# A hybrid decoder layer in three-way split fp32 on one core: first weight blocks between the tiles of x, parameter rows and gates moved ahead, another split of the last sum

## The chip, the core and the metric

One Trainium2 chip, of which the program uses one core. The time is the device time of one execution in microseconds (us), the median over the runs shown; lower is better.

## What is computed

One decoder layer on x (512 x 1024, fp32), followed by a final RMSNorm. Three mixers share one input projection; then come an output projection, a gated MLP with a causal convolution, and the norm.

```python
h = rms_norm(x, attn_norm_w[i])
g_q, g_k, g_v, g_z, g_b, g_a, s_u, d_q, d_k, d_v = split_cols(h @ w_in[i], IN_SIZES)
qkv = jax.nn.silu(causal_dwconv(jnp.concatenate([g_q, g_k, g_v], axis=-1), gdn_conv_w[i]))
...
log_decay = (-jnp.exp(gdn_a_log[i]) * jax.nn.softplus(g_a + gdn_dt_bias[i]))
o_gdn = gated_delta_chunked(l2norm(g_q), l2norm(g_k), g_v, beta, log_decay)   # gated DeltaNet, 4 heads
...
# s5_mixer: per group, s_t = Lbar s_{t-1} + Bbar u_t, y_t = Re(C s_t) + D u_t; GELU; GLU
lam_bar = jnp.exp(lam * dt)
b_bar = ((lam_bar - 1.0) / lam)[..., None] * lax.complex(b_re, b_im)
...
x = x + jnp.concatenate([o_gdn, o_s5, o_diff], axis=-1) @ w_out[i]
x = x + conv_glu_ffn(rms_norm(x, ffn_norm_w[i]), ffn_w_up[i], ffn_conv_w[i], ffn_conv_b[i], ffn_w_down[i])
return rms_norm(x, final_norm_w)
```

## The kernel before

Every fp32 product is three matmuls (`mm3`): both factors are split into a high part (fp32r) and the rest, and high x high, high x low and low x high are summed in PSUM. A weight block of 128 x 512 floats arrives by DMA as `wraw`; ScalarE (ACT) casts it to `whi` (L566), VectorE (DVE) subtracts to get `wlo` (L263), both ahead of the matmuls that use them. Activations are kept feature by token, so the sum of a projection for 128 columns and 512 tokens is one PSUM bank, `acc`.

What happens first, in the order of the text: x arrives in four tiles of 128 tokens (`xt`, L284 to L292). Each tile gets its sum of squares on ACT (`norm_tile`, L1378), a power on GpSimd (POOL), the scaling on DVE (`scale_tile`, L1388, tile `hn`), and transposes on TensorE (PE, `turn`). The transposed halves are evicted from PSUM by ACT (`hi_part`, L1401, tile `hT`) and DVE (`lo_part`, L1404). Four weight blocks (`first_raw`, L1412) feed the first products, for the input u of the S5 mixer. Meanwhile the small parameter vectors come as rows and are turned into columns by PE: `first_params` (L332), `second_params` (L340) and `more_params` (L351; its last piece gives `pl`, the products of the lambda vectors, of which a matmul takes the sum). `s5_tables` (L405) computes the powers of lambda on DVE, with POOL building `ee` and `bm` from `b_nat` and the table `fi`; `more_loads` (L298) issues the loads of `b_nat`, `c_nat`, the convolution rows and so on. The gates of the DeltaNet mixer (`gdn_gates` L892, `gdn_decays` L912) take their 8 columns of w_in from `graw`, and end in `gg`, with its parts `ghi` and `glo`. From those ACT makes eight masked copies `gm` (L1023), and PE sums them into the decays (`gp`). `kq` is the convolved key or query row of a head (`conv_silu`, L958): a scaling on ACT, three shifted multiply-adds on DVE and a product with the tanh `thc`.

What happens last: `last_group` (L1755) adds the last FFN products to x2 in 8 pieces of 128 tokens x 512 columns (j is the half, t the tile), takes the sum of squares on ACT (L1781), accumulates the mean on DVE (`ms`), takes the power on POOL (`rs`), scales half of the columns on DVE (L1794) and half on ACT (L1795), and stores. The last piece is summed in two chunks, so that the first can be added while the second is summed.

The order of each queue is fixed in two ways. PE's follows the program text. For DVE, ACT, POOL and the DMA queue (SP issues every transfer), a table of numbers, `SEQUENCE` (L53 to L133), says in which order the instructions of the text are issued; `in_order` (L135) ties each to the one before it. So an engine never overtakes: an instruction that waits holds all behind it on its engine. There are eight DMA semaphores in turn, so that a DMA issue also waits until the transfer eight issues before it has landed.

Of the kernel before, what the change touches and what calls it, by code (L numbers as in the profile page):

```python
# [12 lines left out]
ALU = mybir.AluOpType  # L13
# [5 lines left out]
D = 1024  # L19
# [35 lines left out]
104-105 129 128 0-1 3 2 92 5 4 35 8 36 76 37 77 38 78 86 6 39 79 40 80 42 7 43-48 41 81 49 82 50 83 51-52 9-11 53 12  # L55
54 13-14 55 84 253 56 85 15 57 65 58 66 59 16-34 60 67 61 68 62 69 63 70 64 71 165 72 74 73 87 75 93 88 90 94 89 97
95-96 91 107 98 166 189 99 101 106 100 130 102 132 131 103 109 133 108 134-135 110 151 136 111-112 137-138 113 141
114-115 142 116 155 139 117-118 143 119 140 147 144 152 126 148 220 145 167 146 149-150 156 127 153-154 168 157-158
# [93 lines left out]
def hybrid_trunk(ctx: ExitStack, tc: tile.TileContext, I: dict, out: bass.AP):  # L152
# [1276 lines left out]
    for b in range(4):  # L1429
        first_raw(b)  # L1430
# [410 lines left out]
```

## Time and profile before

| | |
|---|---|
| three runs, median (lowest to highest) | 821.4 us (819.46 to 824.12) |
| the profiled execution | 822.96 us, span 820.8 us |
| mean granted clock of TensorE | 0.979 |
| PE busy | 788.9 us, 96% of the span |
| DVE busy | 560.9 us, 68% |
| ACT busy | 430.8 us, 52% |
| POOL busy | 103.1 us, 13% |
| HBM | 66.51 MB read, 4.19 MB written |

The span runs from the first to the last instruction. A line such as L263 is that of the helper that records the operation, so groups are told apart by their tiles: `wlo<-wraw,whi` is a weight subtraction. In a timeline, a number in brackets is the time the engine was idle ahead of the instruction, and behind the arrow stands what ended it; `x4` means four instructions merged, from the first start to the last end. Instructions of one engine overlap, so the next one can start before the duration shown is over.

### The profile page before, as it was taken

How to read it: one execution, taken by the hardware profiler on the slowest of the kernel's cores; microseconds unless marked ns; L12 is line 12 of the kernel's file. 1: busy time of each engine (PE TensorE's matmuls, PEld its weight loads, DVE VectorE, ACT ScalarE, POOL GpSimd, SP SyncE). 2: the span in 40 equal slices, each digit the busy share in tenths (PEclk: the TensorE clock that was granted, in tenths of full speed). 3: DMA queues.
4: the chain of work that ended last, by engine and by line, in shares of the span. 5: the costliest groups of instructions: out<-in, count | busy, mean ns of one | idle time of the engine just before them, and what ended most of it. 6: DMA issues, size and time to landing. Idle time of an engine off the chain costs nothing.

```text
span 820.8 us, 13688 instructions
## 1 busy us (share of the span) xinstructions
PE 788.9 (96%) x5004; PEld 649.6 (79%) x5004; DVE 560.9 (68%) x1159; ACT 430.8 (52%) x1001; POOL 103.1 (13%) x133
## 2 busy tenths in 40 slices
PE   7979998998999999999999999999999999999996
PEld 6767887986778878687777788788888888888885
DVE  8898999846657966447357966767466656657635
ACT  5266466645477947586547744444244244335423
POOL 5610000100001201010003111011001001001101
PEclk8998999999999999999999999999999999999999
DMA  6776464378381742341314532333333333333202
GB/s 159 84 116 46 91 92 90 60 112 74 71 65 27 50 79 61 96 82 37 90 49 144 180 90 78 115 101 93 100 93 96 98 91 102 101 92 102 79 1 103
DMA packets 133562, 71.58 MB, mean 87 GB/s; under 512 B 12766, under 2 KB 129784, under 8 KB 133496
## 3 DMA queue, kind: packets, MB, share of 16 engines
q1 hardware_dynamic: 133496, 70.72, 41.5%
q8 instruction: 39, 0.64, 0.3%
q14 instruction: 27, 0.22, 0.1%
HBM read 66.51 MB, written 4.19 MB: 86 GB/s over the span
## 4 chain that ended last, share of the span: by engine, by line
PE 77%; DVE 8%; DMA 7%; ACT 4%; issue 2%; SPq 1%; POOL 1%; POOLq 0%; DVEq 0%; ACTq 0%
PE acc L182 65%; PE gp L182 5%; PE sp L182 5%; DMA wraw<-in_w_in_dram 4%; PE sp L185 1%; DVE wlo L263 1%; PE gp L185 1%; DVE kq L269 1%; DMA wraw<-in_w_out_dram 1%; DMA yf<-swap 1%; DMA swap<-yu 1%; ACT whi L566 1%; PE acc L1608 0%; SPq L696 0%; ACT yh L884 0%
## 5 line engine op out<-in xcount | busy, mean ns | idle before, releaser
L182 PE MATMUL acc<-h,whi 128*128 128x512 f32 x704 | 217.7, 390 | 0.0
L566 ACT CAST whi<-wraw 128x512 fp32r<-128x512 f32 (+2 forms) x224 | 133.4, 597 | 159.5 <-PE acc L182 134.8
L263 DVE TENSOR_TENSOR wlo<-wraw,whi 128x512 fp32r<-128x512 f32 (+2 forms) x224 | 152.4, 682 | 54.0 <-ACT whi L566 46.9
L182 PEld LDWEIGHTS acc<-h,whi 128*128 128x128 f32 x704 | 132.1, 188 | 28.9 <-issue 0.9
L182 PE MATMUL acc<-hT,whi 128*128 128x512 f32 (+1 forms) x464 | 150.0, 400 | 1.2 <-DVE kq L269 1.2
L182 PE MATMUL acc<-h,wlo 128*128 128x512 f32 x352 | 137.0, 390 | 0.0
L182 PEld LDWEIGHTS acc<-hT,whi 128*128 128x128 f32 x464 | 86.1, 193 | 16.1 <-issue 1.6
L182 PE MATMUL acc<-hT,wlo 128*128 128x512 f32 (+1 forms) x240 | 90.9, 390 | 0.0
L263 DVE TENSOR_TENSOR x<-x,acc 128x512 f32<-128x512 f32 (+1 forms) x65 | 44.0, 677 | 57.2 <-PE acc L182 57.2
L182 PEld LDWEIGHTS acc<-h,wlo 128*128 128x128 f32 x352 | 66.1, 188 | 14.0 <-DVE wlo L263 0.3
L269 DVE SCALAR_TENSOR_TENSOR ac<-us,rt,ac 128x511 f32<-128x511 f32 x88 | 65.9, 750 | 13.1 <-ACT ac L1720 11.7
L263 POOL TENSOR_TENSOR ac<-ac 128x512 f32<-128x512 f32 x22 | 35.3, 1606 | 281.0 <-DVE ac L269 199.3
L182 PE MATMUL acc<-ah,whi 128*128 128x512 f32 x144 | 57.5, 400 | 0.1
L182 PE MATMUL acc<-ah,wlo 128*128 128x512 f32 x144 | 56.5, 392 | 0.0
L182 PE MATMUL acc<-al,whi 128*128 128x512 f32 x144 | 56.0, 389 | 0.0
L401 POOL TENSOR_TENSOR rs<-ms,expo 128x4 f32<-128x4 f32 (+1 forms) x14 | 18.8, 1346 | 267.1 <-DVE ms L400 266.9
L182 PEld LDWEIGHTS acc<-hT,wlo 128*128 128x128 f32 x240 | 45.1, 192 | 7.4 <-POOL wlo L1427 0.2
L263 DVE TENSOR_TENSOR us<-acc,rb 128x512 f32<-128x512 f32 x44 | 30.2, 688 | 26.2 <-PE acc L182 26.1
L1720 ACT ACTIVATE ac<-us,rt 128x512 f32<-128x512 f32 x44 | 36.0, 817 | 23.1 <-DVE us L263 23.0
L263 DVE TENSOR_TENSOR al<-ac,ah 128x512 fp32r<-128x512 f32 x22 | 15.2, 691 | 29.9 <-ACT ah L1734 29.3
L1734 ACT CAST ah<-ac 128x512 fp32r<-128x512 f32 x22 | 13.7, 621 | 36.8 <-POOL ac L263 36.8
L182 PEld LDWEIGHTS acc<-ah,whi 128*128 128x128 f32 x144 | 27.1, 188 | 6.7 <-issue 1.1
(567 smaller groups left out, 1401.5 us busy)
## 6 DMA issues: line engine op xcount, KB each, us to landing
wraw<-in_ffn_w_up_dram SPq DMA_DIRECT2D x88, 256.0 KB
wraw<-in_w_in_dram SPq DMA_DIRECT2D x64, 256.0 KB
wraw<-in_ffn_w_down_dram SPq DMA_DIRECT2D x32, 256.0 KB
wraw<-in_w_out_dram SPq DMA_DIRECT2D x24, 128.0 KB
xt<-in_x_dram SPq DMA_DIRECT2D x4, 512.0 KB
xj<-in_x_dram SPq DMA_DIRECT2D x8, 256.0 KB
wraw<-in_w_out_dram SPq DMA_DIRECT2D x8, 256.0 KB
lwraw<-in_ffn_w_down_dram SPq DMA_DIRECT2D x8, 256.0 KB
```

Of the source, the lines that this page charges most:

```text
L182: pe(T.matmul(o, l, r, start=start, stop=stop))
L185: pe(T.transpose(o, i, ident_))
L263: e.tensor_tensor(o, a, b, op=op)
L269: e.scalar_tensor_tensor(o, a, s, b, op0=op0, op1=op1, **kw)
L401: ins = G.tensor_tensor(rs[:, :n], ms[:, :n], expo[:, :n], op=ALU.pow)
L566: S.copy(hi[:, :n], raw[:, :n])
L1720: S.activation(a, us, AF.Identity, scale=fcw(2, f), bias=fcb(f))
L1734: S.copy(ah[:, j, :], up)
```

## The change

1. Tiles 2 and 3 of x are issued between the first weight blocks, which come in the order 0, 2, 1, 3. `wfirst` becomes a dictionary.
2. The row copy and transpose of `second_params` are issued right behind the norm of tile 0; the norms of tiles 2 and 3 are placed behind the first evictions and products. `first_hi`, `first_lo` and `steps` follow them. In PE's order only the four early transposes of tile 2 move, behind the first four matmuls.
3. The cast of `ident_r` is put under program order, and DVE's, ACT's, POOL's and SP's tables are new for the first part of the program (DVE: some 240 instructions); behind it they are the same or exchange near neighbours.
4. The last sum is cut at 384 columns and no longer at 256; the scaling of tile 2 waits in a list until that of tile 3 (`late`, `put`), tile 3 gives 640 columns to DVE and 384 to ACT, and the Squares keep program order.

```diff
@@ loads of x
     dma(small[96:112, 0:32], I["s5_d"][0].rearrange("(q h) -> q h", h=32))
-    dma(xt[:, 2, :], x_v[:, 2, :])
-    dma(xt[:, 3, :], x_v[:, 3, :])
@@ first weights
-    for b in range(4):
+    for b, t in ((0, None), (2, 2), (1, 3), (3, None)):
         first_raw(b)
+        if t is not None:
+            dma(xt[:, t, :], x_v[:, t, :])
@@ first products
     norm_tile(0)
-    next(tabs_)
+    second_params()
     scale_tile(0)
     norm_tile(1)
     next(tabs_)
     scale_tile(1)
-    norm_tile(2)
-    second_params()
-    scale_tile(2)
-    norm_tile(3)
     turn(0, range(KD))
     turn(1, range(KD))
-    turn(2, EARLY)
     first_hi(0, S)
     first_lo(0)
-    scale_tile(3)
+    next(tabs_)
     for k in range(4):
         hi_part(0, k)
+    norm_tile(2)
     first_hi(2, V)
     for k in range(4, 6):
         hi_part(0, k)
+    scale_tile(2)
     steps(0, 5)
+    turn(2, EARLY)
+    first_lo(2)
+    first_hi(1, V)
+    steps(1, 5)
+    norm_tile(3)
+    scale_tile(3)
     turn(3, EARLY)
-    first_hi(1, V)
-    first_lo(2)
-    steps(1, 5)
@@ masks
-        V.tensor_copy(ident_r, ident)
+        keep(V.tensor_copy(ident_r, ident))
@@ last_group
+        def put(t, r):
+            c = 640 if t == NT - 1 else 512
+            xa, xb = x2[:, t, 0:c], x2[:, t, c:D]
+            V.tensor_scalar(xa, xa, r, None, op0=ALU.mult)
+            keep(S.activation(xb, xb, AF.Copy, scale=r))
+            dma(o_v[:, t, 0:c], xa)
+            dma(o_v[:, t, c:D], xb)
...
-            cut = (0, 256, 512) if (j, t) == (1, NT - 1) else (0, 512)
+            cut = (0, 384, 512) if (j, t) == (1, NT - 1) else (0, 512)
...
-                    S.activation(scr[:, c0:c1], xs, AF.Square, accum_out=s)
+                    keep(S.activation(scr[:, c0:c1], xs, AF.Square, accum_out=s))
...
-                V.tensor_scalar(x2[:, t, 0:512], x2[:, t, 0:512], r, None, op0=ALU.mult)
-                S.activation(xs, xs, AF.Copy, scale=r)
-                for k in range(2):
-                    dma(o_v[:, t, 512 * k : 512 * k + 512], x2[:, t, 512 * k : 512 * k + 512])
+                late.append((t, r))
+
+                while late and t != NT - 2:
+                    put(*late.pop(0))
```

Of the table `SEQUENCE` a few entries of the first lines, for the kind:

```diff
     "vector": """
-104-105 129 128 0-1 3 2 92 5 4 35 8 36 76 37 77 38 78 86 6 39 79 40 80 42 7 43-48 41 81 49 82 50 83 51-52 9-11 53 12
+104-105 129 0-3 7 9 8 92 35 11 36 76 37 77 38 78 86 39 79 40 80 42 4-6 43-48 41 81 49 82 10 50 83 253 51 84 52 85 53
...
     "sync": """
-9-12 14-15 13 16-17 19-23 32-33 40 34 41 57-58 35 42 59 36 38 43 37 39 44 26-29 60 24-25 30-31 61-62 47-50 63 52-53
+9-15 17-32 57 33-41 58 42-44 59-60 47-48 61 49-50 52 62 51 53-56 63-66 72 78-82 67-71 83 73-77 89-90 96-97 103 84-85
```

What the new tables make of three places follows. A line is that of its own kernel (in the changed one, two less than before in the middle). First the DMA queue: before, the loads of x and behind them the first four weights, and much later, at a weight block, b_nat.

```order
L288 DMA xt<-in_x_dram 128x1024
L291 DMA xt<-in_x_dram 128x1024
L292 DMA xt<-in_x_dram 128x1024
L1418 DMA wraw<-in_w_in_dram 128x4x128 x4
L299 DMA rows<-in_gdn_conv_w_dram 48x128
...
L564 DMA wraw<-in_w_in_dram 128x4x128
L300 DMA b_nat<-in_s_b_re_dram 128x16x16
L301 DMA b_nat<-in_s_b_im_dram 128x16x16
```

And in the changed kernel, in one row:

```order
L288 DMA xt<-in_x_dram 128x1024
L289 DMA rows<-in_attn_norm_w_dram 8x128
L290 DMA small<-in_s_d_dram 16x32
L1416 DMA wraw<-in_w_in_dram 128x4x128 x2
L1431 DMA xt<-in_x_dram 128x1024
L1416 DMA wraw<-in_w_in_dram 128x4x128
L1431 DMA xt<-in_x_dram 128x1024
L1416 DMA wraw<-in_w_in_dram 128x4x128
L297 DMA rows<-in_gdn_conv_w_dram 48x128
L298 DMA b_nat<-in_s_b_re_dram 128x16x16
L299 DMA b_nat<-in_s_b_im_dram 128x16x16
```

b_nat moved ahead of c_nat, graw and every weight block behind the first four. Next DVE around `pl`. Before, where `pl` and the first uses of `bm` stand:

```order
L357 COPY rt<-sp 128x242
L358 COPY rt<-sp 64x4
L263 TENSOR_TENSOR ct<-pw,bm 128x192
L263 TENSOR_TENSOR pl<-rt 64x2
L263 TENSOR_TENSOR wn<-pw,bm 128x192 x2
```

and, 40 rows later, the end of the gates behind both kq convolutions:

```order
L269 SCALAR_TENSOR_TENSOR kq<-thc,kq 128x512
L263 TENSOR_TENSOR gt<-gt,gmx 128x16
L263 TENSOR_TENSOR cs<-cs,ct 128x512
L269 SCALAR_TENSOR_TENSOR gg<-gt,al 128x16
L263 TENSOR_TENSOR z<-sp,cs 128x512
L945 CAST ghi<-gg 128x16
```

In the changed kernel, first the first use of `bm`, then, 50 rows later, `pl`, the end of the gates and the first kq operation:

```order
L263 TENSOR_TENSOR wlo<-wraw,whi 128x512
L263 TENSOR_TENSOR t<-pw 128x16
L263 TENSOR_TENSOR t_452<-pw 128x16
L263 TENSOR_TENSOR wn<-pw,bm 128x192
...
L263 TENSOR_TENSOR pl<-rt 64x2
L269 SCALAR_TENSOR_TENSOR gt<-gt,gs 128x16
L263 TENSOR_TENSOR ct<-pw,bm 128x192
L263 TENSOR_TENSOR gt<-gt,gmx 128x16
L263 TENSOR_TENSOR cs<-cs,ct 128x512
L269 SCALAR_TENSOR_TENSOR gg<-gt,al 128x16
L263 TENSOR_TENSOR ct<-pw,bm 128x192
L943 CAST ghi<-gg 128x16
```

`bm` is used ahead of `pl` now, and the gates end right behind `pl`. Last, ACT in the tail; before, the scaling of tile 2 (the first L1795 row here) stands ahead of the last Square:

```order
L1781 ACTIVATE scr_8522,ss_8339<-x_5620 128x512
L1781 ACTIVATE scr_8545,ss_8339<-x_5620 128x256
L1795 ACTIVATE x_5620<-x_5620,rs_8341 128x512
L1781 ACTIVATE scr_8562,ss_8339<-x_5620 128x256
L1795 ACTIVATE x_5620<-x_5620,rs_8341 128x512
```

and in the changed kernel both scalings stand behind it:

```order
L1792 ACTIVATE scr_8522,ss_8339<-x_5620 128x512
L1792 ACTIVATE scr_8541,ss_8339<-x_5620 128x384
L1792 ACTIVATE scr_8558,ss_8339<-x_5620 128x128
L1769 ACTIVATE x_5620<-x_5620,rs_8341 128x512
L1769 ACTIVATE x_5620<-x_5620,rs_8341 128x384
```

The last Square no longer stands behind a scaling.

## Rows read from the trace of the kernel before

**Rows 1.** The page's part 4, the chain of work that ended last: shares of the span by engine.

```profile
PE 77%; DVE 8%; DMA 7%; ACT 4%; issue 2%; SPq 1%; POOL 1%; POOLq 0%; DVEq 0%; ACTq 0%
```

**Rows 2.** Timeline of PE, 12 to 66 us. Columns: start in us, duration in us, engine, line, operation, tile out<-in, count, in brackets the idle time before it and what ended it.

```profile
12.15 0.34 PE L185 MATMUL sp<-ident,rows 48*128 48x48 f32 x1 [3.86 <-DVE rows L341]
...
44.52 0.38 PE L182 MATMUL sp<-pl,ones 64*128 64x2 f32 x2 [3.38 <-DVE pl L263]
...
57.80 1.95 PE L182 MATMUL sp<-u,wt 128*128 128x128 f32 x16
61.48 0.36 PE L182 MATMUL gp<-gg,m_ge 128*128 128x16 f32 x2 [1.73 <-DVE gg L269]
...
63.38 0.80 PE L182 MATMUL gp<-gm,m_ltr 128*128 128x512 f32 x1 [1.09 <-ACT gm L1023]
64.55 0.80 PE L182 MATMUL gp<-gm,m_ltr 128*128 128x512 f32 x1 [0.38 <-ACT gm L1023]
65.14 0.63 PE L182 MATMUL gp<-ident_r,negm_r 128*128 128x512 f32 x1
65.56 1.06 PE L185 MATMUL gp<-ident,kq 128*128 128x128 f32 x4
```

**Rows 3.** Stretches of the span (start:end, length in us, busy us and number of instructions of each engine, granted clock of TensorE as a share of full speed, busy share of the 16 DMA engines, GB/s).

```profile
4.00:8.00 4.00, 2.98 (x23) 2.76 (x23) 3.56 (x18) 2.41 (x6) 2.01 (x6) 1.00 0.88 299
31.70:38.50 6.80, 6.80 (x34) 4.60 (x33) 4.64 (x41) 1.20 (x2) 0.02 (x1) 1.00 0.89 92
62.57:69.40 6.83, 5.65 (x20) 4.77 (x21) 6.83 (x16) 5.02 (x22) 0.00 (x0) 0.50 0.95 43
65.50:122.00 56.50, 56.50 (x592) 49.60 (x591) 51.92 (x117) 31.30 (x85) 1.70 (x1) 0.97 0.56 77
243.48:250.31 6.83, 6.83 (x28) 6.08 (x27) 3.94 (x9) 5.05 (x15) 2.05 (x2) 0.50 0.14 42
```

**Rows 4.** Timeline of DVE, 9 to 62 us, columns as in rows 2.

```profile
9.41 0.55 DVE L411 TENSOR_SCALAR yf<-th 128x16 f32<-128x16 f32 x6
...
11.03 0.74 DVE L1390 TENSOR_SCALAR hn<-xt,rs 128x1024 f32<-128x1024 f32 x1
...
15.52 0.74 DVE L1390 TENSOR_SCALAR hn<-xt,rs 128x1024 f32<-128x1024 f32 x1
...
21.51 2.43 DVE L1407 SCALAR_TENSOR_TENSOR hT<-sp,rt,hT 128x256 fp32r<-128x256 f32 x6
...
28.30 0.28 DVE L263 TENSOR_TENSOR yf<-yf 128x128 f32<-128x128 f32 x1
...
38.18 0.69 DVE L263 TENSOR_TENSOR wlo<-wraw,whi 128x512 fp32r<-128x512 f32 x1 [2.16 <-ACT whi L566]
38.79 0.71 DVE L263 TENSOR_TENSOR yf<-gb,yf 128x128 f32<-128x128 f32 x1
...
44.32 0.14 DVE L263 TENSOR_TENSOR pl<-rt 64x2 f32<-64x2 f32 x1
44.39 0.61 DVE L263 TENSOR_TENSOR wn<-pw,bm 128x192 f32<-128x192 f32 x2
...
47.07 0.68 DVE L263 TENSOR_TENSOR cs<-fa,gb 128x512 f32<-128x512 f32 x1
...
61.85 0.16 DVE L945 CAST ghi<-gg 128x16 fp32r<-128x16 f32 x1
```

**Rows 5.** Timeline of ACT, 9 to 64 us.

```profile
9.86 1.06 ACT L1380 ACTIVATE hx<-xt 128x1024 f32<-128x1024 f32 x1 [0.27 <-DMA xt<-in_x_dram]
...
15.49 1.20 ACT L1402 ACTIVATE hT<-gp,rt 128x256 fp32r<-128x256 f32 x3 [3.01 <-PE gp L185]
...
37.53 0.62 ACT L566 CAST whi<-wraw 128x512 fp32r<-128x512 f32 x1 [2.74 <-DMA wraw<-in_w_in_dram]
...
62.05 1.28 ACT L1023 ACTIVATE gm<-m_ge,ghi 128x128 fp32r<-128x128 f32 x4 [1.17 <-DVE ghi L945]
```

**Rows 6.** Timeline of the DMA queue (SP), its issues at 31 to 38 us; the duration is that of the issue, waits included.

```profile
31.18 0.45 SPq L564 DMA_DIRECT2D wraw<-in_w_in_dram  x1
...
32.22 5.08 SPq L301 DMA_DIRECT2D b_nat<-in_s_b_im_dram  x1
```

**Rows 7.** Timeline of POOL, 14 to 43 us and at the end.

```profile
14.18 1.38 POOL L1427 TENSOR_TENSOR wlo<-wraw,whi 128x512 fp32r<-128x512 f32 x1
...
38.48 0.87 POOL L263 TENSOR_TENSOR ee<-b_nat,fi 128x256 f32<-128x256 f32 x1 [7.17 <-DMA b_nat<-in_s_b_re_dram]
...
41.40 1.54 POOL L263 TENSOR_TENSOR bm<-ee 128x256 f32<-128x256 f32 x2
...
815.62 0.92 POOL L263 TENSOR_TENSOR rs<-ms,expo 128x1 f32<-128x1 f32 x1 [1.43 <-DVE ms L269]
```

**Rows 8.** Timeline of DVE at the end.

```profile
812.65 0.42 DVE L263 TENSOR_TENSOR x<-x,acc 128x256 f32<-128x256 f32 x1 [0.35 <-PE acc L182]
...
813.11 0.69 DVE L263 TENSOR_TENSOR x<-x,fw 128x512 f32<-128x512 f32 x1
...
816.58 0.49 DVE L1794 TENSOR_SCALAR x<-x,rs 128x512 f32<-128x512 f32 x1 [0.44 <-POOL rs L263]
```

**Rows 9.** Timeline of ACT at the end.

```profile
814.23 0.72 ACT L1795 ACTIVATE x<-x,rs 128x512 f32<-128x512 f32 x1 [0.56 <-POOL rs L263]
814.86 0.40 ACT L1781 ACTIVATE scr<-x 128x256 f32<-128x256 f32 x1
```

More of the change, by code (lines that the diff above doesn't have):

```diff
@@ new lines @@
+87 54 93 55 94 56 95 57 65 58 66 59 67 12-13 60 68 61 14-16 62 69 63 70 17-30 64 71 31-34 72 74 73 75 88 126 90 89
+130 97 96 91 107 98 106 132 99 101 131 100 133 102 134-135 103 109 136 108 165 110 137 111-112 141 113 138 151
+114-115 142 116 155 166 117-118 204 119 207 205 208 189 206 209 139-140 143-144 147 152 148 156 220 167 145 169 146
+170 149 171 150 153 172 154 157 173 158 161 174 221 175 159 176 160 177 127 178 162 179 128 180 163 181 164 182 198
+190-191 183 199 195 184 242 185 200 186 245 187 241 226 188 244 216 243 217 246 218 201-202 219 203 272 222 168 120
@@ new lines @@
+347 370 378 348 350 371 349 351 396 413 389 388 391 390 414 392 192 196 393 193 197 380 317 194 416 382-384 372 419
+394 397 395 385-386 398-400 415 401-403 405 404 406-407 420 408-409 411 410 412 424-425 417 387 418 461 426 463 421
+460 462 427 422 428-429 434 423 435 440 430-432 441 433 436-437 458 438-439 442 459 443 456 455 457 444-448 468
+449-452 477 453 464 454 469 482 465 470 466 471 467 472 476 473-475 487 498 478-480 483 481 500 484-485 488 486
+489-490 493 491-492 494 496 503 495 497 506 499 511 501-502 522 504-505 507 538 508-509 512 510 542 513-515 541 516
@@ new lines @@
+306 332 304 307 311-312 309-310 313 334 331 314 333 352-353 315-316 354 317 355 318 344 320-322 326 323 327 347 335
+330 324 336 325 342 337 356-357 343 361-362 358-359 338-341 363 345 364 328 348-349 393 365-368 346 360 350-351
+370-373 396 374-375 386 376-378 384-385 387 379-381 388 369 391 389-390 408 392 382 394-395 404 383 406 399 397-398
+403 415 405 400-401 419 402 407 409-410 420 411-414 416 426 417 427 418 421-425 429 432 461-462 457-460 443 428
+430-431 446 435 433-434 436 452 437 440-441 438-439 444-445 453 442 489 491 449 488 490 455 447 450 448 456 451 454
@@ L117 @@
[L117 to L120 removed]
+634 633 644 637 636 645 640 639 646 643 642 647 653-654 869 648 870-871 649 872 656 650 873-874 651 875-876 657 661
@@ L131 @@
+104 86-88 105-106 91-95 112-113 98-102 114-118 107-110 119 111 120-123 128-195 200-219 223-225 348-351 226 352-355
+227-347 356-363
 """,
@@ L1407, in lo_part @@
         keep(V.scalar_tensor_tensor(h_lo(k)[:, hs], half(j, k), anw(k), hi, op0=ALU.mult, op1=ALU.subtract))
-    wfirst = []
+    wfirst = {}
     def first_raw(b):
@@ L1765, in last_group @@
         ]
+        late = []
         for j, t in [(j, t) for j in range(2) for t in range(NT)]:
```

102 lines of the change are left out of this document (42 added, 60 removed).

## Prediction, before the changed kernel was run

> **What bounds the kernel now.** I read the chain that ended last first: 77% of it is TensorE [rows 1]. Through most of the span PE runs one matmul behind the other, so an edit pays only where PE stands idle, where its clock is low, or behind its last matmul. I then read PE's timeline for idle time in front of an instruction, in brackets with what ended it: 3.86 us ahead of the second parameter transpose at 12.15, 3.38 us ahead of the matmul on pl at 44.52, and 1.73, 1.09 and 0.38 us ahead of the gate matmuls at 61.48, 63.38 and 64.55 [rows 2]. The stages give the clock: 0.50 from 62.57 to 69.40, thus 1.2 GHz right behind those idle pieces, 0.97 over 65.5 to 122, and once more 0.50 from 243.48 to 250.31 with PE busy in it [rows 3]. VectorE (DVE) is busy 51.92 of the 56.50 us from 65.5 on, so it is the next bound there [rows 3].
>
> Who makes PE wait? The gate matmuls wait for gg and, through ACT's gm, for ghi, which DVE reaches at 61.85, behind both kq convolutions in its queue [rows 4, 5]. The pl wait ends when DVE gets to pl at 44.32 [rows 4]. On its way DVE lost 2.16 us to a weight cast on ACT (38.18), which itself waited 2.74 us for a weight block [rows 4, 5]; that block was issued only at 31.18 [rows 6]. Then it ran stretched operations beside POOL: 128x128 products took 0.71 us at 38.79, against 0.28 us at 28.30 [rows 4]. POOL works there on ee and bm, having waited 7.17 us for b_nat [rows 7].
>
> **Part 1, first phase (x tiles between weights, parameter rows ahead).** The PE program is the same but for four transposes, so its work costs nothing new. The second parameter transpose no longer waits at 12.15. But ACT's queue now has the Squares of x tiles 2 and 3 behind four and six evictions of hT. Working: tile 1 is scaled about where it was, from 11.03 on [rows 4]; with its transposes the evictions begin near 12.7; six of them at 0.4 us (three took 1.20) and two Squares at 1.06, with some 0.2 us each for the sum's read, follow [rows 5]: 12.7 + 2.4 + 2.5 = 17.6; then mean, power and, ahead of it on POOL, a weight subtraction of 1.38 us [rows 7]: tile 3 is scaled near 19.3, where before it was at 15.52 [rows 4]. The first products start 2 to 3 us earlier than before and then wait for these tiles. I take PE to come to the end of this phase **2 us later** than before, at 43.2 instead of 41.14 (44.52 less the 3.38 of idle time [rows 2]). This costs nothing, because there PE waits for pl; the cover is the old 3.38 us plus the 0.8 us slip of pl below, 4.2 us in all. A phase later than that costs microsecond for microsecond. The bounds of PE's slip by the nearest rows are 0 and 3.8 us (that of tile 3), both inside the cover.
>
> **Part 2, the way to pl.** b_nat, whose second half was issued at 32.22 before [rows 6], now goes out right behind the first weights, so it should be there when POOL gets to it. POOL took 38.48 to 42.94 for ee and bm, 4.46 us [rows 7]. The same six operations now begin when DVE has the fi table. Behind the scaling of tile 3 (to 20.0) its queue holds sixteen low parts of hT at 0.4 (six took 2.43), two dozen small and eight 128-column operations and a cast: some 10.7 us by [rows 4], so POOL begins near **30.7** and bm is there at **35.2**. DVE's first use of bm now stands *ahead of* pl and of the weight subtractions, so DVE stands still there for some 2 us, everything else queued behind. From that row to pl are 55 instructions: 16-column ones at 0.08 (six in 0.55), 192-column ones at 0.27 (two from 44.39 to 44.93), 512-column ones at 0.60 (47.07 to 47.67), the others between, 9.9 us in all [rows 4]. So pl ends at 45.1 and PE, 0.2 behind it as before, goes on at **45.3, 0.8 us later** than 44.52. The stretching beside POOL (0.71 against 0.28 [rows 4]) now falls on other DVE operations, near 31 to 35: at that ratio DVE does in POOL's 4.46 us the work of 1.8, a loss of 2.7, of which 2 lie in its stall anyway; up to 0.7 us is left, which I don't take and keep in the range. The Trainium skill, SBUF — State Buffer, section on the two separate sides, calls it an exclusive lock: a VectorE operation with two SBUF inputs and a GpSimd operation that reads SBUF exclude each other for a whole instruction. By it DVE could lose all 4.46 and the sum would be 818.9; the trace agrees with a stretching, though 0.71 is less than the 0.87 of the POOL operation beside it.
>
> **Part 3, the gates.** From 44.52 PE runs to 59.75 (57.80 + 1.95) without idle: 15.23 us [rows 2]. From 45.3 this ends at 60.5. gg, ghi and glo now stand ahead of all kq convolutions, directly behind pl, so they are done near 47 and ACT's eight gm copies (1.28 us for four [rows 5]) near 50, ten before PE asks. The waits of 1.73, 1.09 and 0.38 us go. What is left is work: 0.8 us for the gg matmuls (61.48 to 63.38, less 1.09), and at half clock 0.8 + 0.6 + 0.42 from 63.38 to 65.56 [rows 2], half of that at full clock, 0.9. The kq transposes start at 60.5 + 0.8 + 0.9 = **62.2 instead of 65.56: -3.4 us**. With no idle ahead of it I expect the stretch at 1.2 GHz to be gone: 65.56 to 69.40 is 3.84 us at half clock, up to **-1.9 us** more (nothing, if the clock stays low). DVE's own queue follows: it drops the 2.16 us wait and the stretching at 38 to 43, pays 2 us at bm, and by the same count of its rows kq is ready near 57.6, ahead of PE.
>
> **Part 4, the tail.** Chunks of 384 and 128 columns replace two of 256. PE's part is hidden: the last add now stands in DVE's queue behind the first chunk's ms, which needs the Square of 384 columns. DVE: fw of tile 2 from 813.11, 0.61 us; add of 384 to 814.3 (between the 0.42 for 256 and 0.69 for 512) [rows 8]; Square and read on ACT to 815.0; ms; add and Square of 128 with read to 815.8 (0.28, 0.28 and 0.18, by the 0.40 that the Square of 256 took [rows 9] less its columns' share); ms and the power on POOL, 0.92 [rows 7], to 817.0, where before the scaling began at 816.58 [rows 8, 9]. The scaling itself, 640 columns on DVE (0.61) and 384 on ACT (0.57), ends 0.1 us sooner than ACT's 0.72 did. What it saves, the Square's wait for ACT's scaling of tile 2 (814.23 to 814.86 [rows 9]), is eaten by the serial order. **+0.4 us**; bounds -0.4 (the Square's saved wait alone) and +0.6.
>
> **Sum.** -3.4 - 1.9 + 0.4 = **-4.9**. The profiled execution took 822.96 us around its span of 820.8, 1.6 over the median; a like execution would come to 818.1, and on the median of 821.4 the forecast is **816.5**. At nothing I put the ident_r cast (it now lies among the 55 instructions, counted there), and the later place of the convolution rows and lambdas on the queue, whose transposes PE reaches only at the end of the first phase; were they late, pl would be, at one for one.
>
> **Rivals.** *C, DVE gives it back.* Behind 65.5 DVE is 92% busy; if its queue gains only the 2.16 us that it no longer waits for ACT, PE meets DVE's lateness in the delta-rule chain. Then 821.4 - 2.2 + 0.4 = 819.6. For it speak the 51.92 of 56.50 [rows 3]; against it that PE ran through 65.5 to 122 without idle, 56.50 of 56.50 [rows 3].
>
> *B, bm comes no sooner (the other side).* b_nat is read in 64-byte pieces, and while such pieces went, 31.7 to 38.5, the DMA engines were 0.89 busy for 92 GB/s, against 0.88 for 299 GB/s with x tiles at 4 to 8 [rows 3]. Now they stand ahead of graw and of the next weight blocks, and DVE has put its first use of bm in front of pl. If bm is ready at 42.9 as before, PE goes on at 42.9 + 9.9 + 0.2 = 53.0, the kq transposes start at 53.0 + 15.23 + 0.8 + 0.9 = 69.9, 4.4 late: 821.4 + 4.4 + 0.4 less up to 1.9 of clock = 824.3 to 826.2, so about **825**. It turns from gain to loss at bm later than 40.0 (27.0 us of fixed work ahead of 65.56 + 1.9 - 0.4). The Trainium skill, DMA: Bandwidth & Descriptors, "Why small descriptors are slow (HBM only)", speaks against this order too: each piece pays a fixed cost on the bus, so 64-byte pieces in front delay all behind; the trace agrees in the direction (92 against 299 GB/s). Against B: from its new place to POOL's turn near 30.7 b_nat has some 15 us, where 6.8 were enough before.
>
> *D, more is gained.* PE's other stretches at 1.2 GHz move or vanish, as the one at 243.48 (6.83 us, worth up to 3.4 [rows 3]): 812 to 814. As well they may arise elsewhere, which is in the range.
>
> *E, the first phase slips past its cover*, say 6 us instead of 2: 1.8 past the 4.2 us, and the clock's 1.9 lost: 816.5 + 3.7 = 820.2.
>
> **How the numbers follow.** Forecast 0.42, C 0.28, B 0.15, D 0.10, E 0.05. About 0.5%, 4.1 us, is what a measurement of this kernel can tell from no change (its runs lay between 819.46 and 824.12): faster is below 817.3, slower above 825.5. The forecast's own spread (clock gain 0 to 1.9, stretching 0.7, tail -0.8 to +0.2 around it) is 814.5 to 818.5, with all but a few hundredths of its chance below 817.3; with D that makes faster 0.48. Some 0.09 of B lies above 825.5: slower 0.09, same 0.43. The range takes in D's cases and stops short of most of B: 811.5 to 824, which leaves out some 0.15.
>
> **What would show it.** Right: no wait of PE at gg or gm, clock 1.0 behind it, kq transposes near 62; POOL's bm near 35, a DVE stall of about 2 us ahead of it; pl near 45; tile 3 scaled near 19; the last scaling 0.4 us later behind PE's last matmul. Wrong: bm past 40, a PE wait in front of gg still, or PE waiting for DVE between 65 and 122 by what was gained.

## The result, and the profile after

The changed kernel is slower: median 830.9 us (four runs, 828.89 to 831.13) against 822.61 for the kernel before beside it; ratio **1.0142, 95% interval [1.0106, 1.0178]**, which is some 11.6 us. The two medians lie only 8.3 us apart (1.010), below that interval; why the ratio is higher, the runs listed do not show, so the size is less certain than the direction. The forecast was 816.5, and the whole range lay below the result. The profiled execution of after took 828.89 us, span 827.0, granted clock 0.977.

The chain that ended last reads as before [rows 1]:

```profile
PE 78%; DVE 8%; DMA 6%; ACT 4%; issue 2%; SPq 1%; POOL 1%; POOLq 0%; ACTq 0%; DVEq 0%
```

PE around pl and the gates, after (columns as in [rows 2]):

```profile
50.66 0.38 PE L182 MATMUL sp<-pl,ones 64*128 64x2 f32 x2 [2.24 <-DVE pl L263]
...
65.75 0.29 PE L182 MATMUL gp<-gg,m_ge 128*128 128x16 f32 x2
...
66.34 0.70 PE L182 MATMUL gp<-gm,m_ltr 128*128 128x512 f32 x2
...
67.12 0.60 PE L185 MATMUL gp<-ident,kq 128*128 128x128 f32 x4
...
68.80 0.71 PE L182 MATMUL acc<-hT,whi 128*128 128x512 f32 x2
```

The stretch behind the gates, and the next one (columns as in [rows 3]):

```profile
62.57:69.40 6.83, 6.83 (x51) 6.29 (x50) 6.69 (x18) 5.31 (x23) 0.00 (x0) 1.00 0.99 44
65.50:122.00 56.50, 53.84 (x590) 47.29 (x589) 53.23 (x116) 30.76 (x84) 2.43 (x1) 1.00 0.51 77
```

The gates did what was forecast: no wait at gg and gm, clock 1.00 where it was 0.50. But PE came to pl at 50.66, 6.1 us late, so all of that was used up: the first acc matmul behind the gates stands at 68.80, against 68.84 before (and 66.30 in a second profile of the kernel before, of which more below). And from 65.5 to 122 PE now has 2.7 us of idle time where it had none.

Where the 6.1 us come from: DVE, ACT, POOL and the DMA queue up to bm (answering to [rows 4 to 7]).

```profile
10.34 0.74 DVE L1388 TENSOR_SCALAR hn<-xt,rs 128x1024 f32<-128x1024 f32 x1
...
12.60 1.75 DVE L1388 TENSOR_SCALAR hn<-xt,rs 128x1024 f32<-128x1024 f32 x1 [0.17 <-POOL rs L1382]
...
19.41 1.76 DVE L1388 TENSOR_SCALAR hn<-xt,rs 128x1024 f32<-128x1024 f32 x1
...
22.30 1.76 DVE L1388 TENSOR_SCALAR hn<-xt,rs 128x1024 f32<-128x1024 f32 x1
```

```profile
10.46 0.62 ACT L1421 CAST whi<-wraw 128x512 fp32r<-128x512 f32 x1 [1.12 <-DMA wraw<-in_w_in_dram]
10.99 0.21 ACT L427 ACTIVATE r<-xr 128x16 f32<-128x16 f32 x1
15.76 1.20 ACT L1400 ACTIVATE hT<-gp,rt 128x256 fp32r<-128x256 f32 x3 [4.57 <-PE gp L185]
...
17.20 1.07 ACT L1378 ACTIVATE hx<-xt 128x1024 f32<-128x1024 f32 x1
...
18.95 1.08 ACT L1378 ACTIVATE hx<-xt 128x1024 f32<-128x1024 f32 x1
```

```profile
11.26 0.61 POOL L644 COPY yf<-r 128x512 f32<-128x512 f32 x1 [4.29 <-ACT r L427]
...
12.54 1.26 POOL L1425 TENSOR_TENSOR wlo<-wraw,whi 128x512 fp32r<-128x512 f32 x1
...
19.26 1.35 POOL L1425 TENSOR_TENSOR wlo<-wraw,whi 128x512 fp32r<-128x512 f32 x1
...
22.17 1.34 POOL L1425 TENSOR_TENSOR wlo<-wraw,whi 128x512 fp32r<-128x512 f32 x1
...
36.84 1.50 POOL L263 TENSOR_TENSOR bm<-ee 128x256 f32<-128x256 f32 x2
```

```profile
11.64 6.40 SPq L299 DMA_DIRECT2D b_nat<-in_s_b_im_dram  x1
...
22.25 0.38 SPq L895 DMA_DIRECT2D graw<-in_w_in_dram  x1
```

Tile 3 is scaled at 22.30 instead of 15.52, three scalings last 1.75 us instead of 0.74, each begun beside a wlo of POOL, and bm is there at 38.34.

The clock has a part in it too. PE's last wait for a scaling ends at 24.11; from there it works without idle, but at half clock. The changed kernel first, then the same stretch of the kernel before (columns as in [rows 3]):

```profile
24.11:28.00 3.89, 3.89 (x18) 3.89 (x19) 3.89 (x11) 1.57 (x4) 1.96 (x6) 0.50 0.25 38
24.11:28.00 3.89, 3.89 (x29) 3.64 (x28) 3.40 (x14) 0.21 (x1) 3.77 (x11) 1.00 0.91 64
```

At full clock PE's work of these 3.89 us would take half as long, so PE might be up to 1.9 us sooner at 28 us (an estimate from these rows; DVE is busy through all of it too, and may then have held PE).

Behind 69 us PE has waits that were not there before, or were shorter (0.98 us at the second, 0.36 at the third); four rows of its timeline, and the rows of DVE and ACT ahead of two of them:

```profile
100.75 0.38 PE L182 MATMUL acc<-whi,hT 128*128 128x256 f32 x1 [2.15 <-ACT up L702]
...
137.75 1.94 PE L182 MATMUL sp<-cmx,wnx 128*128 128x32 f32 x16 [1.96 <-DVE yu L269]
...
242.38 0.43 PE L182 MATMUL gp<-xc,f__2898 32*32 32x32 f32 x8 [2.14 <-ACT yc L1176]
...
289.03 0.45 PE L182 MATMUL gp<-t__3441,lct 32*32 32x32 f32 x32 [3.13 <-DVE t__3441 L263]
```

```profile
285.14 1.23 DVE L1308 TENSOR_REDUCE dsm<-sp 128x2 f32<-128x1024 f32 x1 [0.49 <-PE sp L182]
...
287.97 0.69 DVE L263 TENSOR_TENSOR kl<-dqk,ka 64x512 fp32r<-64x512 f32 x1
288.69 0.29 DVE L263 TENSOR_TENSOR t__3441<-ic,xc 128x128 f32<-128x128 f32 x1
```

```profile
241.42 0.62 ACT L564 CAST whi<-wraw 128x512 fp32r<-128x512 f32 x1 [1.91 <-DMA wraw<-in_w_in_dram]
242.06 0.27 ACT L1176 ACTIVATE yc<-gp 32x128 f32<-32x128 f32 x1
```

In the kernel before, t__3441 stood ahead of the TENSOR_REDUCE (at 282.68), and yc ahead of the cast whi. These are exchanged neighbours of the "later" part of the tables.

The end (answering to [rows 8, 9]): the last scaling on DVE and on ACT begins 2.8 us behind PE's last matmul, in both kernels.

```profile
822.67 0.55 DVE L1768 TENSOR_SCALAR x<-x,rs 128x640 f32<-128x640 f32 x1 [0.44 <-POOL rs L263]
```

### The profile page after: what moved, and what is told of

Its sections match the earlier page's. It is cut to its first block, busy times and chain, and to the rows that moved or that the text cites. A ratio compares the mean times of both kernels' runs of the same rounds, so it can differ in the third digit from the quotient of the medians.

```text
span 827.0 us, 13684 instructions
## 1 busy us (share of the span) xinstructions
PE 789.4 (95%) x5004; PEld 649.1 (78%) x5004; DVE 560.3 (68%) x1159; ACT 429.6 (52%) x1001; POOL 102.2 (12%) x133
## 3 DMA queue, kind: packets, MB, share of 16 engines
HBM read 66.51 MB, written 4.19 MB: 85 GB/s over the span
## 4 chain that ended last, share of the span: by engine, by line
PE 78%; DVE 8%; DMA 6%; ACT 4%; issue 2%; SPq 1%; POOL 1%; POOLq 0%; ACTq 0%; DVEq 0%
PE acc L182 65%; PE gp L182 5%; PE sp L182 4%; DMA wraw<-in_w_in_dram 4%; PE sp L185 2%; DVE wlo L263 1%; DMA swap<-yu 1%; PE gp L185 1%; DVE z L263 1%; DMA wraw<-in_w_out_dram 1%; DVE hn L1388 1%; ACT whi L564 1%; ACT gm L1021 0%; DVE ct L263 0%; DMA yf<-swap 0%
## 5 line engine op out<-in xcount | busy, mean ns | idle before, releaser
L263 DVE TENSOR_TENSOR wlo<-wraw,whi 128x512 fp32r<-128x512 f32 (+2 forms) x224 | 151.8, 679 | 53.1 <-ACT whi L564 45.1
L182 PE MATMUL acc<-hT,whi 128*128 128x512 f32 (+1 forms) x464 | 152.1, 405 | 1.4 <-DVE kq L269 1.4
```

Source lines behind the costliest of these rows:

```text
L182: pe(T.matmul(o, l, r, start=start, stop=stop))
L263: e.tensor_tensor(o, a, b, op=op)
```

## The experiments

Ratios are to the kernel before on the same chip, with 95% intervals; 1% is 8.2 us, and us behind a ratio are worked out from it. "Lead" and "late" are PE's at the same instruction against the kernel before, in its second profile (before_again) where nothing else is said.

| run | what | ratio | first acc behind the gates, us |
|---|---|---|---|
| late_undone | after, old order behind 69 us | 1.0031 [1.0001, 1.0060] | 68.89 |
| late_only | before, new order behind 69 us | 1.0112 [1.0067, 1.0156] | 67.07 |
| kl_site | before, one place of it | 1.0047 [1.0024, 1.0070] | 66.87 |
| queue_site | before, another place | 1.0053 [1.0026, 1.0079] | 65.73 |
| tail_only | before, new tail | 0.9995 [0.9964, 1.0026] | 66.30 |
| before_again | before, one run (820.14 us) | | 66.30 |
| first_alone | before, new first phase and tail | 1.0112 [1.0085, 1.0139] | 73.05 |
| first_restored | before, new order from 26 to 69 us | 1.0025 [0.9993, 1.0056] | 66.33 |
| gates_only | before, gates ahead | 1.0001 [0.9981, 1.0021] | 64.25 |
| gates_two | the same, two waits mended | 1.0002 [0.9978, 1.0026] | 59.27 |
| gates_three | the same, DVE reordered behind | 1.0011 [0.9983, 1.0040] | 58.92 |
| first_lo_dve | after, wlo of first blocks on DVE (one run, 828.82 us) | | 67.32 |
| squares_first | first_alone, Squares early | 1.0164 [1.0128, 1.0199] | 76.60 |
| squares_and_loads | the same, x tiles ahead of weights | 1.0114 [1.0084, 1.0145] | 74.82 |
| loads_first | first_alone, x tiles ahead of weights | 1.0121 [1.0084, 1.0157] | 76.23 |

**Where the late waits come from.** late_undone takes the new tables up to 69 us and the old order behind; late_only is its complement in the kernel before.

> The changed kernel, with the old order of the four queues behind about 69 us (DVE from the second scan of z on, ACT from the casts behind the delta rule's norms, the DMA queue from the fifteenth weight block of w_in behind the first four); first phase, gates and tail stay as changed. Theory L (the exchanged neighbours behind 69 us cost the time: PE's new waits of 2.15 us at 98, 1.0 at 135, 2.14 at 240 and 3.13 at 286): these waits go, the kernel is 5 to 7 us faster than the changed one and within 1.5 us of the kernel before. Rival F (the first phase's slip of 7.6 us leaves DVE and the DMA queue late, and that makes the waits): no more than 1.5 us faster than the changed one, 5 us or more over the kernel before.

> The kernel before, with the new order of the queues behind about 69 us alone; first phase, gates and tail as before. Theory L: 4 to 8 us slower than the kernel before, with PE waits of 2 us near 98, 2 near 238 and 3 near 283. Rival F: within 1.5 us of it, without those waits.

The two ratios, 0.31% and 1.12%, add up to the 1.42% of the change. late_undone gained more than expected (9.1 us on the change, by the ratios) and stayed 2.5 us over the kernel before instead of within 1.5. Against the first profile of before it was 0.05 us late at 69 us; against the second, 2.6 us there and 2.7 at PE's last matmul. Of the four waits it had none above the size of before. late_only had the waits for t__3441 (3.1 us), up (2.3), yu (1.9) and yc (1.9) though nothing in front of them was late. So these waits belong to the order itself. The next two runs take two single places of it, the first in DVE's table, with 21 entries of ACT's beside it (574 is t__3441, 589 the TENSOR_REDUCE, 598 and 600 are kl, 570 and 571 lct), the second in SP's (82 is a weight block, 67 to 70 the swaps of yu):

```diff
-584 570 585 601 571 586 572-574 589 575 593 598 597 594 599 590 595 591 603 592 596 600
+584 601 570 585-586 571 589 572 598 573 600 574 590 575 591 597 593 592 603 594 599 595-596
```
```diff
-67-70 82 71 73-74 83 75-76 89 77 90 96-97 103 84-87 104 88 105 91-94 106 95
+82 67-71 83 73-77 89-90 96-97 103 84-85 104 86-88 105-106 91-95
```

> The kernel before with 23 entries of DVE's table and 21 of ACT's exchanged as in the change, near 280 to 290 us alone: kl and the TENSOR_REDUCE ahead of t__3441, the second lct copy behind a ka cast. Theory L (each exchange costs where it stands): PE waits some 3 us for t__3441 near 288 us, nothing changes elsewhere, and PE's last matmul is 2 to 3.5 us later, total +2 to +3.5. Rival F (the exchange costs only in a program that is already displaced): under 0.5 us at that place and at the end.

> The kernel before with 30 entries of the DMA queue's table exchanged as in the change, from 86 to 140 us alone: a weight block ahead of the four swaps of yu, others moved likewise. Theory L: PE waits some 2 us near 98 to 100 us behind up, which waits for the swapped yu, offset +1.5 to +2.5 there, of which part is absorbed by 240 us; total +0.5 to +2.5. Rival: the queue's exchange costs nothing (under 0.5), and the late up comes from the order of ACT or DVE.

PE's waits in these two kernels (the view of waits: engine, line, what it waited for, us in total, times, longest), kl_site and then queue_site:

```profile
PE gp L182 <- DVE t__3441 L263: 3.3, 1, 3.3
```
```profile
PE acc L182 <- ACT up L704: 3.2, 1, 3.2
```

Each exchange brings its own wait, and 0.47% and 0.53%: 3.9 us (2.0 to 5.7 by the interval) and 4.3 us (2.1 to 6.5), together 8.2 of late_only's 9.2 (5.5 to 12.8). How much is left for yu and yc stays open with such intervals. The rivals are out. Both times lie above what was expected, though the intervals reach into it. In queue_site one reason can be seen: behind the wait the granted clock is low, and PE does 17 matmuls where before_again does 30 (columns as in [rows 3], queue_site first).

```profile
99.20:102.50 3.30, 3.30 (x17) 3.30 (x17) 1.28 (x3) 1.14 (x2) 0.00 (x0) 0.50 0.81 172
99.20:102.50 3.30, 3.30 (x30) 3.30 (x30) 2.14 (x4) 1.65 (x3) 0.00 (x0) 1.00 0.52 74
```

PE is 0.9 us ahead in front of the wait, 2.4 late behind it and 4.0 late behind this stretch. At its last matmul 1.4 us of that are left, as the expectation had it; the ratio says more.

**What the tail does.** tail_only has the new `last_group` alone.

> The kernel before, with the new tail alone (384 and 128 columns, 640 and 384 in the last scaling, tile 2 scaled behind the last Square). From PE's last matmul to the end of the span it was 10.0 us before and 10.6 in the changed kernel: 0.4 to 0.6 us slower, by the profile's end. Rival (the Square's saved wait counts): 0.4 us faster.

No difference that the runs can tell. The 10.0 and 10.6 us of the expectation are counted from the last matmul of 512 columns (810.79 before, 816.38 after); from PE's very last one they are 7.06 and 7.12. The trace shows that the forecast's price was in the wrong place (PE's last matmuls):

```profile
808.95 0.33 PE L182 MATMUL acc<-lwlo,ah 128*128 128x384 f32 x1
...
809.36 0.27 PE L182 MATMUL acc<-lwlo,ah 128*128 128x128 f32 x1
809.47 0.27 PE L182 MATMUL acc<-lwhi,al 128*128 128x128 f32 x1
...
810.48 0.28 PE L182 MATMUL acc<-lwhi,al 128*128 128x128 f32 x1
```

From 809.36 a matmul of 128 columns follows the last in 0.11 us; those of 256 columns before did so in 0.12 (24 of them from 811.01 to 813.76). Twelve of 384 and twelve of 128 take 3.29 us from the first start to the last, 24 of 256 take 2.75. PE pays 0.5 us, and from its last matmul on nothing changes (2.78 against 2.82 us to the last scaling).

**Was the profiled execution a usual one?**

> The kernel before once more, for a second profile. Theory T (the profiled execution on which the sum rests was a late one): weight blocks land some 2 us sooner, ACT's cast near 35 to 36 us instead of 37.53, pl at 42 to 43 us instead of 44.52, PE's wait there 1.1 to 1.5 us instead of 3.38, the wait for gg 1.8 to 3.4. Rival: pl at 44 to 45 with a wait over 3 us, and the four kernels with pl at 42.1 to 42.8 differ for another reason.

PE in this second profile of the kernel before:

```profile
41.98 0.38 PE L182 MATMUL sp<-pl,ones 64*128 64x2 f32 x2 [1.16 <-DVE pl L263]
...
58.95 0.37 PE L182 MATMUL gp<-gg,m_ge 128*128 128x16 f32 x2 [3.31 <-DVE gg L269]
...
66.30 1.00 PE L182 MATMUL acc<-hT,whi 128*128 128x512 f32 x2
```

It was not: pl at 41.98 with a wait of 1.16 us, and ACT's cast, at 37.53 in [rows 5], at 34.34 without a wait. late_only, tail_only, kl_site, queue_site and the three gates kernels below, which share this order up to pl, have pl at 42.02 to 42.78 and waits of 1.15 to 1.51. The cover of 3.38 us on which Part 1 rested belonged to one late weight block.

**The first phase.** first_alone has the change's first phase (the first 92 entries of DVE, 25 of ACT, 24 of POOL, 14 of SP), then the order of before.

> The changed kernel's first phase (order of x tiles and weights, parameter rows, norms, first products), then the order of before in all queues: b_nat late, gates behind kq; the tail is that of the change. Theory E (the slip of the first phase is not covered): PE is 7 to 8 us late at 28 us, DVE's tables are late by nearly as much, pl comes at 47 to 50 us and the gate waits of 3.3, 0.5 and 0.4 us stay; acc behind the gates at 71 to 74 us and the total 5 to 8 us over before. Rival (covered, as predicted): pl's wait takes up the slip, acc behind the gates at 67 to 68.5, total within 2 us of before.

Theory E holds in the mechanism: 7.5 us late at 28 us, pl at 49.25, gate waits of 3.31, 0.47 and 0.38 us as expected, acc at 73.05. In all it is 9.2 us, more than the 5 to 8 expected. first_restored is the other half: the first phase of before, the new order from there to 69 us.

> The kernel before, whose queues take the new order only between the first products and 69 us (b_nat early, bm ahead of pl, gates ahead of kq); x tiles, norms and first products as before, behind 69 us and in the tail as before. Theory L and F both: PE reaches pl near 41, the gate waits (3.2 us) and the low clock behind them go, 3 to 6 us faster than the kernel before. Rival C (DVE gives it back behind 65 us): within 1.5 us of it. Rival B (bm late): slower by 3.

This expectation failed: no gain, but 0.25% (-0.6 to 4.6 us) on the kernel before. PE waited 3.05 us for gw at 33.29. Of that little is due to graw's later issue (24.41 instead of 17.04, behind b_nat and c_nat): ACT's cast of gw came at 28.15, in before_again at 27.44. DVE's subtraction gw came at 32.50 instead of 27.72, behind table operations in its queue. ACT then waited 2.51 us for a weight block at 39.27. bm was there at 35.10, but PE came to pl at 49.81, nearly as late as in the change. The gates took that back (66.33 us at acc, before_again 66.30), and no gain was left.

What makes the phase late? first_lo_dve puts `first_lo` on DVE (`V.tensor_tensor` for `G.tensor_tensor`).

> The changed kernel with the four weight subtractions of the first blocks on DVE instead of POOL; the masks are issued behind the last power instead. Theory S (the scalings hn of tiles 1 to 3 took 1.75 us and not 0.74 because POOL ran a weight subtraction beside them): all four hn take 0.74 us. DVE then pays 0.6 us for each subtraction itself, so PE's lateness at 28 us, 7.6 us against before, falls by 0.5 to 2 only. Rival (a scaling that reads PSUM-near or DMA-busy memory is slow for another reason, such as x and weights still landing): hn stays at 1.7.

DVE in first_lo_dve:

```profile
12.64 0.75 DVE L1388 TENSOR_SCALAR hn<-xt,rs 128x1024 f32<-128x1024 f32 x1 [0.38 <-POOL rs L1382]
13.31 0.68 DVE L1425 TENSOR_TENSOR wlo<-wraw,whi 128x512 fp32r<-128x512 f32 x1
...
18.46 0.75 DVE L1388 TENSOR_SCALAR hn<-xt,rs 128x1024 f32<-128x1024 f32 x1
...
21.45 0.80 DVE L1388 TENSOR_SCALAR hn<-xt,rs 128x1024 f32<-128x1024 f32 x1 [0.45 <-POOL rs L1382]
```

The scalings are back at 0.75 to 0.80, and PE is 6.0 us late at 28 us instead of 7.6: POOL's subtraction beside them was the cause of the 1.0 us each, but of 1.6 us of the slip only. Next the Squares' place, and the place of x on the DMA queue:

```diff
 squares_first
     first_hi(0, S)
-    first_lo(0)
     next(tabs_)
+    norm_tile(2)
+    norm_tile(3)
+    scale_tile(2)
+    scale_tile(3)
+    first_lo(0)
 loads_first and squares_and_loads, SP's table
-17-22
+19 21 17-18 20 22
```

> first_alone with one thing changed back: the Squares of tiles 2 and 3 stand in ACT's queue ahead of the evictions of hT and no longer behind four and six of them; mean, power and scaling of both tiles follow at once, the first weight subtraction on POOL behind the powers. x tiles between the weights and the early parameter rows stay. Theory S (the late Squares, with the scalings stretched beside POOL, make the first phase late): tile 3 is scaled by 17 us instead of 22 to 24, PE's lateness at 28 us falls from 7.6 to 0 to 2.5 us, pl comes at 42 to 44.5 us, and the total falls from 9 us over before to 0 to 3 us over. Rival (the DMA order or the late first scaling make it late, tile 0 being scaled at 10.3 instead of 7.8 us): PE stays 5 to 7 us late at 28 us and the total 6 to 9 us over before.

> squares_first with the DMA queue's order of before for x: tiles 2 and 3 ahead of the four weight blocks (which keep the order 0, 2, 1, 3). Theory X (the x tiles, put between the weights, arrive 4 to 6 us later, and that makes the first phase late): the Squares of tiles 2 and 3 wait for no tile past 11 us, tile 3 is scaled by 15 to 17 us, PE is 0 to 2.5 us late at 28 us, pl at 42 to 44.5 us, and the total is 0 to 3 us over before, where squares_first was 13 us over. Rival (the weights, now later, or the late first scaling hold PE as long): 5 us or more over.

> first_alone with the DMA queue's order of before for x alone: tiles 2 and 3 ahead of the weight blocks; the Squares of tiles 2 and 3 stay behind the evictions of hT. Theory X alone (the loads are all of it): PE is 0 to 2.5 us late at 28 us and the total 0 to 3 us over before. Rival S (with the tiles there in time the Squares' place behind the evictions still costs, as worked out in the prediction): tile 3 is scaled at 20 to 22 us, PE 5 to 7 us late at 28 us, total 5 to 8 us over before.

None of the three made the phase shorter: PE is 10.6, 9.0 and 10.3 us late at 28 us, where first_alone has 7.5. In squares_first ACT waits for the tiles, which stand behind two and three weight blocks in the DMA queue:

```profile
13.92 1.06 ACT L1378 ACTIVATE hx<-xt 128x1024 f32<-128x1024 f32 x1 [3.22 <-DMA xt<-in_x_dram]
...
15.97 1.06 ACT L1378 ACTIVATE hx<-xt 128x1024 f32<-128x1024 f32 x1 [0.91 <-DMA xt<-in_x_dram]
```

With the tiles ahead, as in squares_and_loads, the first weight arrives later instead (ACT's cast at 12.76, having waited 4.09 us), and behind that cast in ACT's queue stands r, for which POOL's copy yf waits, and behind yf the power of tile 1: hn of tile 1 moves from 12.60 to 14.87. So the traces point to at least four things in series: the cast ahead of r, the loads, the Squares behind the evictions, and DVE's table operations ahead of the scalings and low parts, and behind them the low clock. Of the versions here only the whole old order gets the time back. The share of each stays open.

**What the gates are worth.** Four kernels have before's first phase and the gate series ahead: first_restored and these three.

```diff
 gates_two, DVE
-198 221 199 216 200 217 245 218 226 172 241 173 219 174 244 175 243 176 246 177 222 178 201 179 223 180 254 181 224 ...
+198 221 199 216 172-173 200 174 217 175-176 245 177 218 178 226 179-180 241 181 244 182 243 183 246 184-185 219 186-187 222 188 ...
```

> The kernel before with one thing of the change: the series that ends in gg, ghi and glo stands ahead of the second kq convolution in DVE's queue, gu and the eight gm copies likewise in ACT's. First phase, b_nat, pl, tables and tail are as before. Theory G (the gates gain what the prediction said, once nothing is late in front of them): pl and PE to 59.75 us stay as before, the waits of 1.73, 1.09 and 0.38 us go and the matmuls behind them run at full clock, so PE starts the kq transposes 3 to 4 us sooner and is 4 to 5.5 us ahead by 69 us; total 4 to 6 us less, some 812 to 815 beside 818 for before. Rival C (DVE's lateness or a new wait behind 69 us takes it back): the same lead at 69 us, but no more than 2 us of it left at PE's last matmul.

> As gates_only, with its two new waits taken out: the gate series is spread between DVE's larger operations from the first kq convolution on and the weight subtraction that PE asked for at 52.3 us is ahead of its end; on ACT the ed copy stands right behind the gm copies and thc, ahead of the copies d. Theory G: in gates_only PE lost 1.63 us to wlo and 2.74 us to ed, so of what the gates gave, little was left (acc behind the gates at 64.25 us, against 65.7 to 67.1 in four kernels that have the order of before there). Without the two waits acc comes at 60 to 61.5 us, and the total falls by 3 to 6 us, some 811.5 to 814.5 where before takes 817.5. Rival C: the lead at 69 us is there, but DVE gives it back before 140 us and the total is within 1.5 us of before.

gates_only lost most of its lead at once, to wlo (1.63 us) and ed (2.74 us), and by 82 us all of it; gates_two kept it: acc at 59.27, 7 us ahead of before_again. PE in gates_two:

```profile
55.83 0.29 PE L182 MATMUL gp<-gg,m_ge 128*128 128x16 f32 x2
...
59.27 0.71 PE L182 MATMUL acc<-hT,whi 128*128 128x512 f32 x2
...
77.58 0.65 PE L182 MATMUL gp<-t__1030,lct 32*32 32x32 f32 x32 [4.19 <-DVE t__1030 L263]
```

Ahead of 77.58 PE stands 4.19 us for t__1030. DVE ends it at 77.53, having waited no more than 1.10 us (for POOL's rs) since 57.40; in before_again it did so at 77.79, where PE asks for it at 79.47 and finds it ready. The gates came sooner, but DVE did not. By 82 us the lead is gone and the total is that of before. gates_three puts DVE's chain to t__1030 ahead of its S5 work.

> gates_two with DVE's queue from 64 to 82 us put in another order: the mean ms, the scalings lt and the chain lct, xc, t__1030 ahead of the S5 operations en, zt, ct and of the vT products, the two lct copies of ACT ahead of its copies d. Theory D (behind the gates DVE is the bound, through the place of t__1030 in its queue): in gates_two PE was 7 us ahead at 59 us and waited 4.19 us for t__1030 at 77.24 us. With t__1030 near 70 us that wait goes, 2.5 to 5 us of the lead are left at 130 us and the total falls by 2 to 5 us, some 813.5 to 816.5 where before takes 818. Rival (DVE's work as a whole is the bound, not its order): PE waits as long for vT, wlo or the next steps of the chain, and the total is within 1.2 us of before.

t__1030 then was ready at 71.6 and PE took it at 72.97, but stood at the next steps:

```profile
77.75 0.65 PE L182 MATMUL gp<-xc,f__1031 32*32 32x32 f32 x32 [3.44 <-DVE xc L263]
79.28 1.19 PE L182 MATMUL acc<-hT,whi 128*128 128x512 f32 x2 [0.88 <-DVE vT L269]
```

xc stood in DVE's queue behind a vT that waited 1.67 us for ACT, so part of this is my order. For the rest, DVE has little room there in before_again (columns as in [rows 3]).

```profile
70.00:120.00 50.00, 49.80 (x556) 43.16 (x555) 47.55 (x105) 26.36 (x62) 0.00 (x0) 1.00 0.50 83
120.00:140.00 20.00, 17.39 (x135) 14.62 (x136) 19.72 (x44) 12.68 (x34) 0.00 (x0) 1.00 0.41 88
```

From 120 to 140 it is busy 19.72 of 20 us, and the same 19.72 in gates_two. That a lead would be spent waiting there as well is read from these shares: no version brought a lead so far. No version here beats the kernel before.

## Why the prediction was wrong

**The step that failed first** is a sentence ahead of the sum: behind the first part the tables "are the same or exchange near neighbours", and the prediction put no price on that. The runs put 9.2 us on it (late_only), and two single places cost 3.9 and 4.3. No mechanism was missing: each could have been read by asking, at every exchanged pair, who waits for the one that moved back.

**Part 1** was mis-sized and its cover was not there. PE was to come to the end of the phase at 43.2; it came at 48.42 (50.66 less 2.24). That "tile 1 is scaled about where it was" failed (12.60 to 14.35 instead of 11.03), so the evictions began at 15.76 and not at 12.7 (they had begun at 15.49 before [rows 5]), and tile 3 was scaled at 22.30 and not at 19.3. I had asked in which queue the Squares stand, not when x lands nor what stands in front of r. The lock of the Trainium skill (SBUF — State Buffer, the two separate sides) was applied to bm alone; the trace shows its effect, 1.0 us, on each scaling begun beside a subtraction. Each of the three ended 0.55 to 0.56 us behind POOL's subtraction (14.35 for 13.80, 21.17 for 20.61, 24.06 for 23.51), as if held until its end. So did the product of 0.71 us that the prediction took for a stretching at a ratio: it ended at 39.50, POOL's operation beside it at 39.35 [rows 4, 7]. Part 1 also put nothing on the clock, which may be worth up to 1.9 us (the estimate above). As to the cover: 3.38 us in one execution, 1.15 to 1.51 in eight others. Rival E was the right mechanism. It was given a chance of 0.05 and 3.7 us over the forecast (1.8 past the cover and 1.9 of clock), where first_alone measures 9.2 us over the kernel before.

**Part 2**: bm at 38.34 instead of 35.2, the end of pl at 50.61 instead of 45.1. POOL began on ee at 34.03 instead of 30.7, which follows tile 3. But the stall of 2 us ahead of bm did not come: DVE reached its first use of bm at 40.01, 1.7 us behind bm, and was busy all of the 12.13 us from 38.34 to pl. So DVE's own queue put pl there, not bm. In front of that use its small operations were slowed beside POOL (a 128x32 product took 0.61 us at 34.74, 0.18 at 35.27), and from it to the end of pl are 10.6 us (forecast 9.9). first_restored shows that this part was mis-sized by itself: with no late first phase bm is there at 35.10, as forecast, and PE still comes to pl at 49.81 instead of 45.3. Rival B's objection, that b_nat delays what stands behind it, shows there as 0.7 us at graw; whether the late weight block is due to it, no run separates.

**Part 3** was right where it looked: waits gone, clock 1.00, 15.09 us from pl to gg (forecast 15.23), and from pl to acc 6.2 us gained (18.14 for 24.32; forecast 6.1, that is 3.4 and 1.9 and the slip of 0.8). Its worth was wrong. In first_restored PE comes to pl 7.8 us later than in before_again and to acc at the same time (66.33 and 66.30), so what the gates give there only makes up for the later pl. Rival C, "DVE gives it back", held at 0.28, is what gates_two shows; I argued against it that PE had no idle time from 65.5 to 122 [rows 3], but that says only that PE was the later of the two by a little. In the displaced program the gates do pay: from first_alone (1.0112) to late_undone (1.0031) is 6.6 us by the ratios. In the traces PE is 4.2 us sooner at t__1030 (81.77 for 85.93), to which the new order brings DVE at 80.50 instead of 83.96.

**Part 4** was right in size by luck (0.5 for 0.4) and wrong in place: "PE's part is hidden", yet PE pays it, and the last scaling is no later behind its last matmul. The runs cannot tell the total from nothing.

The sum by the runs: 9.2 for the first phase, -6.6 for the order up to 69 us, 9.2 for the order behind, 0 for the tail: 11.8 us, where the ratio of the change gives 11.6 and its medians 8.3. The -6.6 is the difference of two ratios (late_undone less first_alone) and holds in the displaced program only. None of the prediction's signs of being wrong came (bm past 40, a wait at gg, PE waiting for DVE between 65 and 122 by what was gained): the loss lay where it had set no sign. Of its signs of being right only the two at the gates came, no wait and the clock.

## What to carry over

An order table is a change at every line in which it differs: price each exchanged pair by its waiters, also far from the edit that was meant. A stretch in which PE never idles does not show that the engine behind has room: compare when each of them reaches the next hand-over. A wait can cost more than its length, where the clock falls behind it (queue_site: 3.2 us of wait, then some 1.6 us at half clock). And a cover read from one execution is worth checking in a second one before it is spent.

## Hardware behaviour that I had not expected

A 128x1024 scaling on DVE took 1.74 to 1.76 us when POOL had begun a 128x512 subtraction 0.06 to 0.15 us before it (after, first_alone, loads_first), and 0.74 to 0.80 otherwise. Where DVE began first (squares_first, hn at 17.94 and wlo at 18.01), hn kept its 0.75 and POOL's took 1.81 instead of 1.26: the second one pays. A matmul of 128 columns cost 0.11 us in a row (tail_only) where one of 256 cost 0.12 (before). Runs of one kernel spread with the granted clock: before's spans on one chip went from 811.7 us at a mean granted clock of 0.988 to 822.0 us at 0.980.
